# Weights' sums partly by DMA, SwiGLU groups of 8, 6, 8, and later first hidden tiles in a two-layer trunk kernel

## The chip, the cores and the metric

The kernel runs on one core of a Trainium2 chip. The metric is the device time of one execution in microseconds, the median of three runs. In this text TensorE is PE in the rows of the profile, VectorE is DVE, ScalarE is ACT, GpSimd is POOL, and SP is the engine whose queue issues most DMAs. T is 528, the 512 tokens with 16 learned meta tokens ahead of them.

## What is computed

Two layers, each a half-step SwiGLU (f1), a mixer (retention in layer 0, gated linear attention, GLA, in layer 1), and another half-step SwiGLU (f2), all in float32:

```python
def swiglu(x, w_in, w_out):
    gate, up = jnp.split(x @ w_in, 2, axis=-1)
    return (jax.nn.silu(gate) * up) @ w_out

for i in range(DEPTH):                      # D_MODEL 1024, D_FF 2816 = 22 tiles of 128
    h = h + 0.5 * swiglu(rmsnorm(h, norm_ffn1[i]), ffn1_w_in[i], ffn1_w_out[i])
    hn = rmsnorm(h, norm_mix[i])
    h = h + (retention if i % 2 == 0 else gla)(hn, ...)
    h = h + 0.5 * swiglu(rmsnorm(h, norm_ffn2[i]), ffn2_w_in[i], ffn2_w_out[i])
h = rmsnorm(h, final_norm)                  # meta tokens are dropped
```

## The kernel before, in words

All activations lie transposed, features on the 128 partitions and tokens along the free axis, in eight residual tiles x[0..7]. Every float32 operand of a matmul is split into a high part (rounded to fp32r) and a low part (the rest), and one product is three matmuls (`mm3`, lines 311 to 313): high x high, high x low, low x high. So each piece of weights of up to 512 columns costs a copy on ScalarE (`whi`, line 121) and a subtraction on VectorE (`wlo`, line 122).

Most of the work is done in units. A unit multiplies two weight tiles with both halves of the tokens in 7 products in place of 8 (Strassen's scheme in Winograd's form). For that, `Weights` takes four quarters of two loaded weight tiles (a11, a12 in the first, a21, a22 in the second) and forms four sums on VectorE (`ws`, line 107): s1 = a21 + a22, s2 = s1 + a11, s3 = a11 + a21, s4 = a12 + s2. The activations get four such sums too (`t_sums`, lines 463 to 466). The order within a unit is a11, s1, s2, a12, s3, s4, a22; the first unit of a SwiGLU begins with s1 and s2. A product runs over nk pairs of tiles, 3 matmuls each: 84 matmuls in a unit with nk = 4, 63 with nk = 3. There are 134 units, 18 input and 12 output units in each of four SwiGLUs and 14 in the retention.

A SwiGLU computes its first four hidden tiles plainly, straight from the entering residual, while the norm's statistics are still on their way (`plain`, `evac`; the norm is applied to the result). Meanwhile VectorE forms the normed tiles and their sums (`norm`, `sums`). Then pairs of tiles follow as a gate unit and an up unit each. `hidden` splits a finished pair of hidden tiles and forms its sums. Hidden tiles are put into groups (8, 8 and 6 of the 22; in the very last SwiGLU 6, 6, 6 and 4). When a group is full, four output units, each for two residual tiles, are put behind the next gate unit; the last group's follow the last up unit at once. In a SwiGLU that feeds a next stage the last group's output units also carry that stage's entry (`feed`): for each residual tile the scaled high part on ScalarE (`uha`, line 382), the low part on VectorE (`ula`, line 384), a square on ScalarE and the sum of squares on VectorE (`sqa`, line 392). The norm's power is taken on GpSimd (`rc`, line 429; in the heads of the mixers `r_ro` and `r_go`, line 356).

Weights are loaded by SP's queue in DMAs of 1024 columns (512 KB) into four buffers, and split ahead into seven pairs of buffers, up to four pieces ahead of the one in use. Buffers, semaphores and the order of the instructions on each engine come from a planner, which simulates the program with its own costs and issues what is ready by priority; the chip then runs each engine's list in that fixed order. A piece of work marked `urgent` is taken earlier.

Of the kernel before, what the change touches and what calls it, by code (L numbers as in the profile page):

```python
# [10 lines left out]
F32 = mybir.dt.float32  # L11
# [5 lines left out]
P = 128  # L17
# [6 lines left out]
T = 528  # L24
# [5 lines left out]
GROUPS = ((0, 8), (8, 16), (16, 22))  # L30
# [15 lines left out]
CW = 1024  # L46
# [8 lines left out]
class Weights:  # L55

    UNIT = ("a11", "s1", "s2", "a12", "s3", "s4", "a22")
    FIRST = ("s1", "s2", "a11", "a12", "s3", "s4", "a22")  # L60
    SUMS = {"s1": ("a21", "a22"), "s2": ("s1", "a11"), "s3": ("a11", "a21"), "s4": ("a12", "s2")}

    def __init__(self, tc, ctx, raw_bufs=4, bufs=7):
        self.nc = tc.nc
        self.raw_pool = ctx.enter_context(tc.tile_pool(name="wraw", bufs=raw_bufs))
        self.pool = ctx.enter_context(tc.tile_pool(name="wsplit", bufs=bufs))
        self.raw_bufs, self.bufs = raw_bufs, bufs
        self.chunks, self.raw = [], {}
        self.plan, self.parts, self.sums = [], {}, {}
        self.loaded = self.done = self.split = self.taken = 0  # L70
        self.live = set()
        self.sum_pool = None

    def add(self, key, ap):
        n = ap.shape[1]
        c = len(self.chunks)
        self.chunks.append(ap)
        for o in range(0, n, PW):
            self.plan.append((key, c, o, min(PW, n - o), o + PW >= n))

    def add_unit(self, key, ap1, ap2, order):
        c = len(self.chunks)
        self.chunks += [ap1, ap2]
        for q in order:
            self.plan.append((key + (q,), c, q, ap1.shape[1] // 2, {"s4": c, "a22": c + 1}.get(q)))

    def _load(self):
        while self.loaded < min(self.done + self.raw_bufs, len(self.chunks)):
            ap = self.chunks[self.loaded]
            t = self.raw_pool.tile([P, CW], F32, tag="raw", name=f"raw{self.loaded}")  # L90
            self.nc.sync.dma_start(t[:, :ap.shape[1]], ap)
            self.raw[self.loaded] = t
            self.loaded += 1

    def _piece(self, c, q):

        V = self.nc.vector
        if not isinstance(q, str):
            return self.raw[c][:, q:q + PW]
        n = self.chunks[c].shape[1] // 2  # L100
        if q[0] == "a":
            o = (int(q[2]) - 1) * n
            return self.raw[c + int(q[1]) - 1][:, o:o + n]
        if (c, q) not in self.sums:
            a, b = [self._piece(c, i) for i in self.SUMS[q]]
            t = self.sum_pool.tile([P, PW], F32, tag="wsum", name=f"w{q}_{c}")[:, :n]
            V.tensor_add(t, a, b)  # L107
            self.sums[c, q] = t
        return self.sums[c, q]

    def _split(self, upto):
        oldest = min(self.live, default=self.taken)
        upto = min(upto, len(self.plan), oldest + self.bufs)
        while self.split < upto:
            i = self.split
            _, c, q, n, last = self.plan[i]
            self._load()
            raw = self._piece(c, q)
            hi = self.pool.tile([P, PW], F32R, tag="hi", name=f"whi{i}")
            lo = self.pool.tile([P, PW], F32R, tag="lo", name=f"wlo{i}")  # L120
            self.nc.scalar.copy(hi[:, :n], raw[:, :n])  # L121
            self.nc.vector.tensor_sub(lo[:, :n], raw[:, :n], hi[:, :n].bitcast(F32))  # L122
            self.parts[i] = (hi, lo)
            self.split += 1
            if last not in (None, False):
                self.raw.pop(c if last is True else last)
                self.done += 1
                self._load()

    def prime(self, n=None):  # L130
        bufs = self.raw_bufs
        self.raw_bufs = n or bufs
        self._load()
        self.raw_bufs = bufs
# [27 lines left out]
def trunk(ctx, tc, a):  # L162
# [28 lines left out]
    def plan_ffn(w_in, w_out, layer, which, last=False):  # L191
        first = True
        for kind, a_, b_ in ffn_steps(last):
# [7 lines left out]
            else:  # L201
                f0, f1 = (LAST_GROUPS if last else GROUPS)[a_]
                c = slice(f0 * P, f1 * P)
                if kind == "o":
                    W.add_unit(key, w_out[layer, b_, :, c], w_out[layer, b_ + 1, :, c], W.UNIT)
                else:
                    W.add(key, w_out[layer, b_, :, c])
# [58 lines left out]
    W.prime(1)  # L266
# [190 lines left out]
    def t_sums(pool, name, halves, y1, y2, hi, lo):  # L457


        (a0, a1), (b0, b1) = halves  # L460
        wd = a1 - a0
        t = pool.tile([P, 4, 264], F32, tag="su", name=f"tt{name}")[:, :, :wd]
        V.tensor_sub(t[:, 0], y1[:, a0:a1], y1[:, b0:b1])
        V.scalar_tensor_tensor(t[:, 1], y2[:, b0:b1], -1.0, t[:, 0], ALU.mult, ALU.subtract)
        V.tensor_sub(t[:, 2], y2[:, b0:b1], y1[:, b0:b1])
        V.scalar_tensor_tensor(t[:, 3], y2[:, a0:a1], -1.0, t[:, 1], ALU.mult, ALU.subtract)
        split(hi[:, :, :wd], lo[:, :, :wd], t)
# [5 lines left out]
    def unit(key, name, first, halves, nk, rhs, pool, row1, c22, c21):  # L473
# [35 lines left out]
    def quarters(halves, th, tl):  # L509
# [3 lines left out]
        def rhs(what, k):  # L513
# [3 lines left out]
            i = ("t1", "t2", "n3", "t4").index(what)  # L517
# [5 lines left out]
    def ffn(which, layer, halves, gcol, feed, late=False):  # L523
# [5 lines left out]
        with tc.tile_pool(name=f"h_{me}", bufs=4) as hp, tc.tile_pool(name=f"t_{me}", bufs=1) as tp, \  # L529
                tc.tile_pool(name=f"u_{me}", bufs=3) as up_, tc.tile_pool(name=f"s_{me}", bufs=4) as sp, \  # L530
# [1056 lines left out]
```

## Time and profile before

| | us |
|---|---|
| median of 3 runs (2143.5 to 2145.68) | 2143.53 |
| the profiled execution | 2141.96 |
| its span, first to last instruction | 2140.2 |
| TensorE busy, matmuls (16950) | 2103.9 |
| VectorE busy (3451 instructions) | 1868.0 |
| ScalarE busy | 1146.0 |
| GpSimd busy (25 instructions) | 21.8 |

The mean granted clock of TensorE was 0.997 of full. The stages, by windows of the span: head and first SwiGLU to 375 us, retention to 820, second SwiGLU to 1170, third to 1528, GLA to 1800, last SwiGLU to the end. Matmuls overlap: the next begins before the one ahead of it has ended, so that TensorE shows as busy although its beat is slower than it could be; the number of matmuls in a window tells more.

### The profile page before, as it was taken

Reading aid. Unit: us, or ns where it says so; the run is one execution under the profiler, and the core shown is the slowest. Engines: PE = TensorE matmul, PEld = TensorE weight load, DVE = VectorE, ACT = ScalarE, POOL = GpSimd, SP = SyncE. Lnnn points to the kernel's source line nnn. Section 1 sums busy time; section 2 is a strip of 40 time slices with the busy share of each in tenths; the row PEclk is TensorE's granted clock in tenths of the full one; section 3 lists DMA queues with packets and bytes.
Section 4 is the critical chain, followed back from the end, with each engine's and each line's share of the span. In section 5 each row is a group of like instructions: output and inputs, shape, how many; then the busy total and the mean of one; then the engine's idle time right before and its main releaser. Section 6 shows DMA issues by size and latency. Waiting matters only on the chain.

```text
span 2140.2 us, 42535 instructions
## 1 busy us (share of the span) xinstructions
PE 2103.9 (98%) x16950; PEld 2069.3 (97%) x16950; DVE 1868.0 (87%) x3451; ACT 1146.0 (54%) x2220; POOL 21.8 (1%) x25
## 2 busy tenths in 40 slices
PE   8999999999999999999999999999999999999998
PEld 7999999999999999999998999999899999999998
DVE  7999999977686879999999999989876658999996
ACT  5656656443434354656566565656733235656654
POOL 0000000000000000000000000000000000000000
PEclk9999999999999999999999999999999999999999
DMA  4333323332222222232323233332312112233332
GB/s 142 98 110 100 103 93 92 100 110 82 97 80 96 83 71 79 90 109 99 109 93 96 80 109 103 97 107 86 122 60 66 63 62 78 87 121 99 104 109 75
DMA packets 59175, 201.26 MB, mean 94 GB/s; under 512 B 6624, under 2 KB 8032, under 8 KB 58976
## 3 DMA queue, kind: packets, MB, share of 16 engines
q1 hardware_dynamic: 57968, 195.26, 28.5%
q10 hardware_dynamic: 1008, 3.29, 0.5%
q8 instruction: 133, 2.18, 0.4%
q14 instruction: 66, 0.54, 0.1%
HBM read 196.42 MB, written 2.10 MB: 93 GB/s over the span
## 4 chain that ended last, share of the span: by engine, by line
PE 79%; DVE 15%; ACT 2%; DMA 2%; issue 2%; POOL 0%; SPq 0%; DVEq 0%; POOLq 0%; ACTq 0%
DVE wlo L122 4%; DVE ws L107 2%; PE po_r L313 1%; PE po_r L311 1%; PE po_r L312 1%; PE lv L1227 1%; DVE hf L340 1%; PE Xf21o L311 1%; PE Xf20o L311 1%; DMA raw<-in_f_in 1%; PE Xf20g L311 1%; PE Xf20g L312 1%; PE Xf20g L313 1%; PE Xf20u L311 1%; PE Xf11g L311 1%
## 5 line engine op out<-in xcount | busy, mean ns | idle before, releaser
L121 ACT CAST whi<-raw 128x512 fp32r<-128x512 f32 (+1 forms) x613 | 369.1, 608 | 393.2 <-PE gv L312 51.0
L121 ACT CAST whi<-ws 128x512 fp32r<-128x512 f32 (+1 forms) x536 | 322.3, 603 | 340.9 <-DVE ws L107 86.8
L122 DVE TENSOR_TENSOR wlo<-raw,whi 128x512 fp32r<-128x512 f32 (+1 forms) x613 | 402.9, 668 | 67.6 <-ACT whi L121 65.8
L122 DVE TENSOR_TENSOR wlo<-ws,whi 128x512 fp32r<-128x512 f32 (+1 forms) x536 | 349.5, 659 | 27.6 <-ACT whi L121 25.5
L107 DVE TENSOR_TENSOR ws<-raw 128x512 f32<-128x512 f32 (+1 forms) x134 | 88.6, 661 | 20.1 <-DMA raw<-in_f_in 13.6
L107 DVE TENSOR_TENSOR ws<-ws,raw 128x512 f32<-128x512 f32 (+1 forms) x134 | 88.6, 661 | 1.6
L107 DVE TENSOR_TENSOR ws<-raw,raw 128x512 f32<-128x512 f32 (+1 forms) x134 | 88.3, 659 | 0.4
L107 DVE TENSOR_TENSOR ws<-raw,ws 128x512 f32<-128x512 f32 (+1 forms) x134 | 88.2, 658 | 0.4
L313 PE MATMUL po_r<-ogh,wlo 128*128 128x264 f32 x256 | 72.9, 285 | 0.0
L311 PE MATMUL po_r<-ogh,whi 128*128 128x264 f32 x256 | 72.9, 285 | 0.0
L312 PE MATMUL po_r<-ogl,whi 128*128 128x264 f32 x256 | 72.6, 284 | 0.0
L339 ACT CAST hf<-yf 128x264 fp32r<-128x264 f32 (+2 forms) x86 | 45.0, 534 | 33.0 <-DVE yf L641 20.3
L311 PE MATMUL Xf10o<-hf,whi 128*128 128x264 f32 x176 | 51.1, 291 | 2.9 <-ACT whi L121 2.7
L311 PE MATMUL Xf11o<-hf,whi 128*128 128x264 f32 x176 | 51.1, 291 | 2.9 <-ACT whi L121 2.7
L311 PE MATMUL Xf20o<-hf,whi 128*128 128x264 f32 x176 | 51.1, 291 | 2.8 <-ACT whi L121 2.7
L313 PE MATMUL Xf20o<-hf,wlo 128*128 128x264 f32 x176 | 50.3, 286 | 0.0
L313 PE MATMUL Xf11o<-hf,wlo 128*128 128x264 f32 x176 | 50.3, 286 | 0.0
L313 PE MATMUL Xf10o<-hf,wlo 128*128 128x264 f32 x176 | 50.3, 286 | 0.0
L312 PE MATMUL Xf10o<-hf,whi 128*128 128x264 f32 x176 | 50.1, 285 | 0.0
L312 PE MATMUL Xf11o<-hf,whi 128*128 128x264 f32 x176 | 50.0, 285 | 0.0
L312 PE MATMUL Xf20o<-hf,whi 128*128 128x264 f32 x176 | 50.0, 285 | 0.0
L340 DVE TENSOR_TENSOR hf<-yf,hf 128x264 fp32r<-128x264 f32 (+2 forms) x86 | 49.3, 573 | 0.6 <-ACT hf L339 0.5
(732 smaller groups left out, 8671.6 us busy)
## 6 DMA issues: line engine op xcount, KB each, us to landing
raw<-in_f_in SPq DMA_DIRECT2D x176, 512.0 KB, 3.5
raw<-in_f_out SPq DMA_DIRECT2D x48, 512.0 KB, 3.6
raw<-in_ret_in SPq DMA_DIRECT2D x48, 512.0 KB, 3.4
raw<-in_f_out SPq DMA_DIRECT2D x48, 384.0 KB, 3.1
raw<-in_gla_in SPq DMA_DIRECT2D x25, 512.0 KB, 3.4
raw<-in_ret_o SPq DMA_DIRECT2D x16, 512.0 KB, 3.4
raw<-in_gla_o SPq DMA_DIRECT2D x8, 512.0 KB, 3.5
xa<-in_xT SPq DMA_DIRECT2D x8, 264.0 KB, 5.3
```

The costliest lines, as they stand in the source:

```text
L107: V.tensor_add(t, a, b)
L121: self.nc.scalar.copy(hi[:, :n], raw[:, :n])
L122: self.nc.vector.tensor_sub(lo[:, :n], raw[:, :n], hi[:, :n].bitcast(F32))
L311: nc.tensor.matmul(ps, lhsT=lh, rhs=rh, start=start, stop=False, **kw)
L312: nc.tensor.matmul(ps, lhsT=lh, rhs=rl, start=False, stop=False, **kw)
L313: nc.tensor.matmul(ps, lhsT=ll, rhs=rh, start=False, stop=stop, **kw)
L339: S.copy(hi, src)
L340: V.tensor_sub(lo, src, hi.bitcast(F32))
L1227: nc.tensor.matmul(ps[:, j, J * P:J * P + n], lhsT=Kt[:, j, J * P:(J + 1) * P], rhs=q, start=(J == 0), stop=(J == 3), skip_group_check=True)
```

## The change

Weights of units are loaded in smaller pieces: the quarters a11, a12 and a22 as tiles of their own (seven buffers of 512 columns), and a pair tile (three buffers) that gets a11 and a22 by SP's queue and then a21 added to both halves by one accumulating DMA of GpSimd's queue. The pair is then s3 and s1. VectorE still forms s2 and s4, in place, right after the split of a11 and a12. A pair is begun no more than three units ahead of the split.

The groups become 8, 6, 8. The last group's first output unit runs its first three products (order a11, s1, a12) over all pairs of tiles but the last, then over the last.

Of the first four, plain hidden tiles, the splits and sums are put behind the next gate units (`todo`). The sums of activations are three instructions in place of four, and a hidden tile is split in two pieces in place of three. Plain weights are loaded in DMAs of 512 columns. The scratch for GpSimd's DMAs is 2048 in place of 4096.

```diff
-GROUPS = ((0, 8), (8, 16), (16, 22))
+GROUPS = ((0, 8), (8, 14), (14, 22))
...
+    LATE = ("a11", "s1", "a12", "s2", "s3", "s4", "a22")
+    def __init__(self, tc, ctx, raw_bufs=7, pair_bufs=3, bufs=7):
...
     def add_unit(self, key, ap1, ap2, order):
+        a = {"a11": ap1[:, :n], "a12": ap1[:, n:], "a21": ap2[:, :n], "a22": ap2[:, n:]}
+        self.loads["pair"].append((c, len(self.plan), (a["a11"], a["a22"], a["a21"])))
+        for q in ("a11", "a12", "a22"):
+            self.loads["raw"].append(((c, q), len(self.plan), (a[q],)))
...
     def _load(self):
+        for kind, loads in self.loads.items():
+            while self.begun[kind] < min(self.over[kind] + self.room[kind], len(loads)):
+                c, first, aps = loads[self.begun[kind]]
+                if kind == "pair" and first > self.split + 3 * len(self.UNIT):
+                    break
+                if kind == "pair":
+                    t = self.pair_pool.tile([P, 2, PW], F32, tag="pair", name=f"pair{c}")[:, :, :n]
+                    for i in range(2):
+                        nc.sync.dma_start(t[:, i], aps[i])
+                    nc.gpsimd.dma_start(t, aps[2].unsqueeze(1).broadcast_to([P, 2, n]), accum_op=ALU.add)
+                else:
+                    t = self.raw_pool.tile([P, PW], F32, tag="raw", name=f"raw{self.begun[kind]}")[:, :n]
+                    nc.sync.dma_start(t, aps[0])
...
     def _split(self, upto):
+                late = order[0] == "s1"
+                s2 = self.tiles[c][:, 1] if late else self.tiles[c, "a11"]
+                raw = {"s1": self.tiles[c][:, 1], "s3": self.tiles[c][:, 0], "s2": s2,
+                       "s4": self.tiles[c, "a12"]}.get(q)
...
+            self.nc.scalar.copy(hi[:, :n], raw)
+            V.tensor_sub(lo[:, :n], raw, hi[:, :n].bitcast(F32))
+                if q == ("s1" if late else "a11"):
+                    V.tensor_add(s2, self.tiles[c][:, 1], self.tiles[c, "a11"])
+                elif q == "a12":
+                    V.tensor_add(raw, raw, s2)
...
-    def t_sums(pool, name, halves, y1, y2, hi, lo):
+    def t_sums(pool, name, b22_b11, b12, b21):
+        V.tensor_sub(t[:, :2], b22_b11, b12.unsqueeze(1).broadcast_to([P, 2, wd]))
+        V.scalar_tensor_tensor(t[:, 2], b22_b11[:, 0], -1.0, t[:, 1], ALU.mult, ALU.subtract)
+        V.scalar_tensor_tensor(t[:, 3], b21, -1.0, t[:, 2], ALU.mult, ALU.subtract)
...
     def unit(key, name, order, halves, nk, rhs, pool, row1, c22, c21):
+        steps = [(q, 0, nk) for q in order]
+        if order == W.LATE:
+            steps = [(q, 0, nk - 1) for q in order[:3]] + [(q, nk - 1, nk) for q in order[:3]] + steps[3:]
...
             def hidden(f, y):
-                    split(hi[:, 4], lo[:, 4], y[:, 0, a0:a1])
-                    t_sums(up_, f"{me}h{f}", halves, y[:, 0], y[:, 1], h[:, 0, :4], h[:, 1, :4])
-                    split(hi[:, 5:], lo[:, 5:], pair(y[:, 1], halves))
+                    t = t_sums(up_, f"{me}h{f}", y[:, 1:3], y[:, 3], y[:, 0])
+                    split(hi[:, :3], lo[:, :3], y[:, :3])
+                    split(hi[:, 3:], lo[:, 3:], t)
...
             def evac(f, outs):
-                    hidden(f - 1, y)
+                    todo.append((f - 1, y))
...
+                    while todo and (a_ == "g" or b_ + 2 == groups[0][1]):
+                        hidden(*todo.popleft())
+                        if a_ == "g":
+                            break
```

## Rows read from the trace of the kernel before

**Rows 1.** The page, busy time and share of the span of each engine.
```profile
PE 2103.9 (98%) x16950; PEld 2069.3 (97%) x16950; DVE 1868.0 (87%) x3451; ACT 1146.0 (54%) x2220; POOL 21.8 (1%) x25
```

**Rows 2.** Windows: width; busy (instructions) of PE, PEld, DVE, ACT, POOL; clock, DMA share, GB/s.
```profile
1340.00:1380.00 40.00, 40.00 (x331) 40.00 (x330) 39.46 (x72) 25.95 (x52) 0.00 (x0) 1.00 0.33 107
2080.00:2100.00 20.00, 20.00 (x172) 20.00 (x171) 17.27 (x30) 12.54 (x26) 0.00 (x0) 1.00 0.28 80
60.00:320.00 260.00, 259.54 (x2113) 257.78 (x2113) 247.46 (x441) 154.37 (x305) 0.00 (x0) 1.00 0.31 100
1200.00:1480.00 280.00, 279.79 (x2281) 278.10 (x2280) 266.86 (x476) 166.67 (x324) 0.00 (x0) 1.00 0.33 102
1800.00:2100.00 300.00, 299.77 (x2506) 297.61 (x2506) 296.07 (x562) 183.38 (x375) 0.00 (x0) 1.00 0.32 99
```

**Rows 3.** Windows in the head, at a group's end and in last output units.
```profile
48.00:62.00 14.00, 9.29 (x53) 8.76 (x53) 12.06 (x24) 4.90 (x7) 0.00 (x0) 0.76 0.25 77
56.00:58.00 2.00, 2.00 (x11) 2.00 (x11) 2.00 (x5) 0.80 (x2) 0.00 (x0) 0.50 0.88 283
336.00:344.00 8.00, 7.37 (x50) 6.28 (x50) 8.00 (x17) 5.47 (x13) 0.00 (x0) 1.00 0.16 50
358.00:370.00 12.00, 9.79 (x70) 8.76 (x70) 11.83 (x24) 7.50 (x17) 0.00 (x0) 1.00 0.28 91
1510.00:1528.00 18.00, 14.67 (x106) 13.18 (x105) 17.71 (x35) 13.49 (x29) 0.00 (x0) 1.00 0.39 121
```

**Rows 4.** Waits: engine and line, whom it waited for, us in total, times, longest.
```profile
ACT whi L121 <- DVE ws L107: 86.8, 69, 3.4
...
PE Xf10o L311 <- ACT whi L121: 2.7, 3, 1.2
```

**Rows 5.** The page's groups of instructions: the sums s1 and s3 on VectorE.
```profile
L107 DVE TENSOR_TENSOR ws<-raw 128x512 f32<-128x512 f32 (+1 forms) x134 | 88.6, 661 | 20.1 <-DMA raw<-in_f_in 13.6
...
L107 DVE TENSOR_TENSOR ws<-raw,raw 128x512 f32<-128x512 f32 (+1 forms) x134 | 88.3, 659 | 0.4
```

**Rows 6.** Groups of instructions on VectorE from 346 to 376 us.
```profile
L384 DVE SCALAR_TENSOR_TENSOR ula<-xa,gains,uha 128x528 fp32r<-128x528 f32 x8 | 6.0, 761 | 0.0
...
L665 DVE SCALAR_TENSOR_TENSOR xa<-QZf10o,xa 128x528 f32<-128x528 f32 x4 | 2.8, 701 | 0.2 <-PE QZf10o L313 0.2
...
L676 DVE SCALAR_TENSOR_TENSOR xa<-Xf10o,xa 128x264 f32<-128x264 f32 x4 | 1.7, 429 | 0.0
```

**Rows 7.** Timeline of VectorE: start, us, line, operation, out<-in.
```profile
355.53 0.70 DVE L392 TENSOR_TENSOR sqa_n<-sqa_n,sq_n 128x528 f32<-128x528 f32 x1
...
358.42 0.55 DVE L107 TENSOR_TENSOR ws<-raw,raw 128x384 f32<-128x384 f32 x1
...
359.82 1.01 DVE L122 TENSOR_TENSOR wlo<-ws,whi 128x384 fp32r<-128x384 f32 x2
...
380.31 1.88 DVE L122 TENSOR_TENSOR wlo<-raw,whi 128x512 fp32r<-128x512 f32 x3
```

**Rows 8.** Timeline of TensorE and VectorE at a group's end, and at 359 us.
```profile
335.94 0.28 PE L313 MATMUL Xf10u<-thf,wlo 128*128 128x264 f32 x1
...
340.40 1.25 DVE L340 TENSOR_TENSOR hf<-ttf10h,hf 128x1056 fp32r<-128x1056 f32 x1
...
341.70 0.19 PEld L312 LDWEIGHTS QZf10o<-hf,whi 128*128 128x128 f32 x1 [0.27 <-DVE hf L340]
...
359.56 0.39 PE L311 MATMUL Xf10o<-hf,whi 128*128 128x264 f32 x1 [1.22 <-ACT whi L121]
```

**Rows 9.** Timeline of VectorE in the head.
```profile
46.54 1.24 DVE L340 TENSOR_TENSOR hf<-ttf10h,hf 128x1056 fp32r<-128x1056 f32 x1
...
51.48 0.68 DVE L122 TENSOR_TENSOR wlo<-raw,whi 128x512 fp32r<-128x512 f32 x1
```

**Rows 10.** The page's DMA issues: count, KB each, median us to landing.
```profile
raw<-in_f_in SPq DMA_DIRECT2D x176, 512.0 KB, 3.5
```

**Rows 11.** Timeline of POOL at the first SwiGLU's end.
```profile
378.20 1.90 POOL L429 TENSOR_TENSOR rc<-ms_n,half_neg 128x4 f32<-128x4 f32 x2 [354.56 <-DVE ms_n L427]
```

More of the change, by code (lines that the diff above doesn't have):

```diff
@@ L66, in __init__ @@
         self.pool = ctx.enter_context(tc.tile_pool(name="wsplit", bufs=bufs))
[L67 to L70, printed above, removed]
+        self.bufs = bufs
+        self.loads = {"raw": [], "pair": []}
+        self.begun = dict.fromkeys(self.loads, 0)
+        self.over = dict.fromkeys(self.loads, 0)
+        self.room = {"raw": raw_bufs, "pair": pair_bufs}
@@ L71, in __init__ @@
+        self.tiles, self.plan, self.parts = {}, [], {}
+        self.split = self.taken = self.keys = 0
         self.live = set()
-        self.sum_pool = None
     def add(self, key, ap):
[L75 to L79, printed above, removed]
-    def add_unit(self, key, ap1, ap2, order):
-        c = len(self.chunks)
-        self.chunks += [ap1, ap2]
+        c = self.keys
@@ L84, in add_unit @@
         for q in order:
-            self.plan.append((key + (q,), c, q, ap1.shape[1] // 2, {"s4": c, "a22": c + 1}.get(q)))
+            self.plan.append((key + (q,), c, q, n, order))
     def _load(self):
[L88 to L93, printed above, removed]
@@ L95, in _piece @@
-    def _piece(self, c, q):
-        V = self.nc.vector
[L98 to L109, printed above, removed]
@@ L204, in plan_ffn @@
                 if kind == "o":
-                    W.add_unit(key, w_out[layer, b_, :, c], w_out[layer, b_ + 1, :, c], W.UNIT)
+                    late = not last and (a_, b_) == (len(GROUPS) - 1, 0)
+                    W.add_unit(key, w_out[layer, b_, :, c], w_out[layer, b_ + 1, :, c], W.LATE if late else W.UNIT)
                 else:
@@ L537, in ffn, with place @@
             groups = GROUPS if feed else LAST_GROUPS
+            def place(j):
+                if j not in normed:
+                    t = hp.tile([P, 4 * T + 4 * 264], F32, tag="H", name=f"un{me}{j}")
+                    normed[j] = t[:, :4 * T].rearrange("p (i h t) -> p i h t", i=2, h=2)
+                    normed[j, "y"] = t[:, 4 * T:].rearrange("p (q t) -> p q t", q=4)
+                return normed[j]
             def norm(j):
-                t = normed[j] = hp.tile([P, 2, 2, T], F32, tag="H", name=f"un{me}{j}")
+                t = place(j)
                 for h in range(2):
@@ L558, in renorm @@
                         k = 4 * h + 2 * j
[L559 removed]
+                        split(uha[:, k:k + 2, r0:r1], ula[:, k:k + 2, r0:r1], normed[j][:, :, 1 - h, r0:r1])
             def gates(f):
@@ L564, in gated @@
             def gated(f):
-                return up_.tile([P, 2, T], F32, tag="su", name=f"y{me}{f}")
+                if f < NPL:
+                    place(f // 2)
+                    return normed[f // 2, "y"][:, :, :wd]
+                return up_.tile([P, 4, 264], F32, tag="su", name=f"y{me}{f}")[:, :, :wd]
             def hidden(f, y):
@@ L571, in hidden @@
                     h = hp.tile([P, 2, 2, T], F32R, tag="H", name=f"h{me}{f}")
-                    split(h[:, 0, :, a0:], h[:, 1, :, a0:], y[:, :, a0:])
+                    for i in range(2):
+                        split(pair(h[:, 0, i, :], halves), pair(h[:, 1, i, :], halves), y[:, 2 - 2 * i:4 - 2 * i])
                 else:
@@ L630, in c21 @@
                     S.activation(g[1][:, a0:a1], c, AF.Silu)
-                unit((which, layer, "i", "g", f), f"{me}g{f}", first, halves, 4, rhs_in, up_, row1, c22, c21)
+                unit((which, layer, "i", "g", f), f"{me}g{f}", W.FIRST if first else W.UNIT, halves, 4, rhs_in, up_,
+                     row1, c22, c21)
                 return g
@@ L678, in c21 @@
                         feed(d + 1, ins)
-                unit((which, layer, "o", gi, d), f"{me}o{gi}{d}", False, halves, len(hs), rhs, up_, row1, c22, c21)
+                late = feed and (gi, d) == (len(groups) - 1, 0)
+                unit((which, layer, "o", gi, d), f"{me}o{gi}{d}", W.LATE if late else W.UNIT, halves, len(hs), rhs,
+                     up_, row1, c22, c21)
             first, ps, outs, g = True, {}, {}, None
```

136 lines of the change are left out of this document (76 added, 60 removed).

## The prediction

> **What bounds the kernel now.** I read the page first: TensorE is busy 98% of the span and VectorE 87% [rows 1]. A busy TensorE is no measure of waste here, since matmuls overlap, so I counted them. In the cleanest stretch that I found, 40 us hold 331 matmuls [rows 2]; one lasts 0.28 us [rows 8], so some 2.3 of those counted only reach over an edge, and the beat is 40 / 328.7 = 0.1217 us for 264 columns. In the last SwiGLU, with 256 columns, 20 us hold 172: 20 / 169.7 = 0.1179 us [rows 2]. The change alters no count of matmuls (the groups are 8, 6, 8 for 8, 8, 6, in all 22 tiles), so all that it can win is time in which the beat is missed: width less (count - 2.3) x beat.
>
> By windows, of three long stretches of SwiGLU units the first (60 to 320) misses 260 - 2110.7 x 0.1217 = 3.1 us and the last (1200 to 1480) 2.7; with as much for the one between them (820 to 1120) and 300 - 2503.7 x 0.1179 = 4.8 us in the last SwiGLU [rows 2] that is 13, spread thin. Short windows give the rest [rows 3]: 7.8 us in the head (48 to 62); 2.2 us where the last group's first output unit begins (336 to 344; there are three such places, the others at 1130 and 1488, so some 6.5 in all); and in the last output units of a SwiGLU that feeds a next stage 3.8 us (358 to 370) and 5.4 (1510 to 1528), with one such place between them some 14 in all. The sum is 7.8 + 6.5 + 14 + 13 = 41 us: 1.9% of the time, and the ceiling.
>
> What ends these misses? The waits name the split of the weights: an output unit's first product waits for the high part, and ScalarE, which makes it, waited 86.8 us for the sums of weights on VectorE [rows 4]. In the short windows VectorE is full (17.71 of 18 us, 11.83 of 12) [rows 3].
>
> **The sums by DMA.** Four sums a unit (s1, s2, s3, s4) become two, since s1 and s3 are now formed as a22 + a21 and a11 + a21 by a DMA that adds to a loaded pair. Taken from VectorE: 134 of each, 88.6 + 88.3 = 177 us of busy time [rows 5]. Instructions in a row overlap a little: three splits of 512 take 1.88 us, so one costs (1.88 - 0.68) / 2 = 0.60 and 268 of them 161 us [rows 5, 7]. In units of 10.2 us (84 matmuls at 0.1217) that is 1.2 us less of VectorE. But there TensorE misses only 1% to 1.6%, so nearly all of the 161 us lies beside other work. Of the 13 us I take back 4 (bounds 0 and 13): short waits for evacuations and splits, of which a VectorE with 12% of air should lose some.
>
> **Groups 8, 6, 8.** In the last group's output units VectorE also carries the next stage's entry. For one unit: two ula at 0.76, two sqa at 0.70, two residual updates of 528 at 0.70, three of 264 at 0.43 [rows 6, 7], each less 0.08 of overlap: 1.36 + 1.24 + 1.24 + 1.05 = 4.9 us. With three pairs the weights are 384 wide; a split or sum costs 1.01 - 0.55 = 0.46 [rows 7], and 7 splits + 4 sums make 5.1. Together 10.0 us, against 63 matmuls x 0.1217 = 7.7 on TensorE: VectorE is 2.3 us short in each of four units, which prefetched splits cover in part, and 14 us in three stages is what is left. The sight of it: squares' sums and weights' sums run at 355.53 and 358.42, and TensorE gets its high part at 359.56, 1.22 us idle [rows 7, 8]. After the change the last group has four pairs: 4.9 + 9 x 0.60 = 10.3 us against the 10.2 of 84 matmuls. The shortage falls from 2.3 to 0.1 us. I take back 11 of 14 us (bounds 0 and 14). The middle group, now of three pairs, pays nothing: without the entry its units ask 2.3 + 9 x 0.46 = 6.4 us of VectorE in 7.7.
>
> **The last group's first unit begun without its last tiles.** Before, the last up-unit's last matmul starts at 335.94, VectorE splits the sums of its hidden tile from 340.40 to 341.65, and TensorE, which ran what it could, waits for them at 341.70 [rows 8]: 5.6 us of chain, of which 2.2 are missed. Merged sums hardly shorten it (four of 0.35 become one of 0.62 and two of 0.35; three splits become two): 0.2 us. The new order runs three products over three of four pairs first, 27 matmuls or 3.3 us, then the fourth pair's two plain products (0.36 each): 4.0 us. If the planner lets s2's first products in as well, the wait goes; if not, 1.6 us stay. I take 1.3 a place, 4 of 6.5 us (0 and 6.5). Its price: three weights must lie split within 3.3 us where one per 1.1 to 1.4 us did; should they be late, it is this gain that goes.
>
> **The first hidden tiles split later.** In the head VectorE does norms, their sums and the first two hidden tiles one behind the other. A weight's low part comes only at 51.48, behind, among others, the hidden tile's split at 46.54 [rows 9], while TensorE stands and its granted clock falls, to a mean of 0.76 over 48 to 62 and to half, the 1.2 GHz level, at 56 [rows 3]. Moving hidden tile 0 behind the first gate unit takes away four sums of 264 (1.4 together, at 0.43 less overlap), splits of 264 and 528 (1.0, at the same prices [rows 6]) and of 1056 (1.2 [rows 9]), some 3.5 us. The stand is about 4.5 us, and the clock's fall follows it; with 1 us left I expect no fall (the wait at 359 left the clock at 1.00 [rows 3]). Back: 5 of 7.8 us (0 and 7.8). The moved work lands in units that have 1.2 us of new air each; three units take it.
>
> **What it adds.** In each of 134 units: two pair loads and three quarters of 256 KB each on SP's queue (less where a unit is 384 wide) in place of two loads of 512 KB, and one accumulating DMA on POOL's queue, that writes 512 KB and reads its source twice. The trace has no such DMA and none from POOL. It waits for its two loads; behind it on POOL stand the next pair's DMA and the small powers of the norms, behind its landing the splits of s1 and s3 on ScalarE and VectorE. Nearest row: 512 KB plain lands in 3.5 us [rows 10]; so the chain of a pair is 3.5 for the loads and between 3.5 and, at five times that, 17 us for the add. Pairs are begun about three units (30 us) ahead, so even 21 us is covered; without that cover each unit would wait. The DMA engines are 0.33 busy in a stretch where a unit loads 1 MB [rows 2]; 1.25 MB plain is 0.41, and the add 0.17 at the plain price, its lower bound: 0.58 at least, full enough to collide. The upper bound is five times that, rival B below; by the nearest row I take the lower one. The Trainium skill ("Collectives: The Full Stack", The bandwidth ceiling: the fold count and why AG ≠ RS ≠ AR) speaks against a cheap add: a DMA that sums reads two sources over one ring, so it moves half of what a copy does. By that rule the add would take 0.33 and the engines would be 0.74 busy, and the time would still be TensorE's; no run here shows its rate yet. Plain weights in DMAs of half the size and the smaller scratch I cost at nothing: they are loaded seven pieces ahead, about 2.9 us of matmuls each, against 3.5 us to land; without that lead a stage's first pieces would wait. For POOL's queue, later loads and a new order of all queues I put 3 us (bounds 0 and 15; a gain is excluded, since nothing is taken from these queues).
>
> **Sum.** 4 + 11 + 4 + 5 - 3 = 21 us. Against the profiled execution: 2141.96 - 21 = 2121.0 (its span is 2140.2, 1.8 us lie around it); the median of the runs is 1.6 us above it, so I forecast 2122.5 us.
>
> **Rivals.** (A) The order hardly changes: VectorE's order is fixed ahead by the planner, which put entry work before weights' splits when both were ready [rows 7]; if it does so again, the freed time lies between stalls and not in them, and I lose most of 11 + 5, leaving some 5 us: 2138.5. For it: VectorE idles almost nowhere in the stalls. Against it: there the demand itself was too high, and that falls. Chance 0.15.
>
> (B) Slower: the add is so dear that the DMA engines bind. It decides where a unit's DMA time passes 10.2 us: 4.2 us plain (0.41 x 10.2) leaves 6.0 for the add, that is 3.5 times its plain 1.7 us. At four times: 4.2 + 6.8 = 11.0, 0.8 us a unit x 134 = 107, less the 21 won: 2230; at five times 2.5 x 134 = 335, and 2458. For it: no row gives an add's rate. Against it: engines at a third. Chance 0.07.
>
> (C) Slower: POOL's queue. A norm's power (two take 1.90 us [rows 11]) stands behind a pair's DMA that waits for its loads, 3.5 us; 14 such norms (6 of stages, 8 of heads), uncovered, are 49 us less the 21: 2143.5 + 28 = 2171. For it: POOL serves in order. Against it: most norms have matmuls under them. Chance 0.06.
>
> **Numbers.** Forecast 0.72. All terms at their best give 41 us back; the three local ones whole (28) and most of the thin 13 give 39, the low end: 2104. (A) is held by a top end of 2140; B and C lie outside (0.13). Within 0.2% (4.3 us) is about what a measurement of this kernel cannot tell from no change: faster than that 0.80, within 0.08 (half of A), slower 0.12.
>
> **What would show it.** Right: two sums a unit on VectorE, its share in the long stretches near 0.84 for 0.95; over 330 matmuls per 40 us in stretches that had fewer; no fall of the clock at 50 us; under 2 us missed in the last units of a stage. Wrong: TensorE or ScalarE waiting for a pair's DMA in mid-stage (B), a POOL power late with matmuls idle (C), or VectorE full with the same waits (A). Shares of DMA above 0.8 would speak for B.

## The result, and the profile after

The changed kernel took 2117.39 us (median of 4 runs, 2117.36 to 2117.42) against 2143.52 for the kernel before (2143.41 to 2145.68): a ratio of 0.9876, with a 95% interval of 0.9864 to 0.9889. The forecast was 2122.5, with a range of 2104 to 2140. The profiled span fell from 2140.2 to 2115.3 us, by 24.9.

The page after: engines, then DMA queues (packets, MB, share of 16 engines' span), and the issues of weights (count, KB, us to landing).

```profile
PE 2090.6 (99%) x16950; PEld 2064.2 (98%) x16950; DVE 1731.8 (82%) x3085; ACT 1143.5 (54%) x2184; POOL 184.7 (9%) x159
...
q1 hardware_dynamic: 130400, 228.84, 33.0%
q0 software_dynamic: 36448, 67.12, 20.0%
...
raw<-in_f_in SPq DMA_DIRECT2D x280, 256.0 KB, 4.0
pair<-in_f_in SPq DMA_DIRECT2D x144, 256.0 KB, 4.6
pair<-in_f_in POOLq DMA_DIRECT2D x72, 512.0 KB, 6.2
```

The count of matmuls is the same as in [rows 1], so again all that was won is time in which the beat is missed: width less (count - 2.3) x 0.1217 us, or x 0.1179 in the last SwiGLU. Windows after, with the columns of [rows 2]: the head; the last output units of the first three SwiGLUs; the three groups' ends; the long stretches of the four SwiGLUs.

```profile
48.00:62.00 14.00, 14.00 (x117) 14.00 (x116) 13.28 (x20) 7.54 (x15) 0.00 (x0) 1.00 0.29 95
338.00:362.00 24.00, 24.00 (x200) 24.00 (x199) 22.52 (x41) 16.28 (x33) 1.21 (x1) 1.00 0.68 172
1128.00:1154.00 26.00, 25.62 (x211) 25.42 (x209) 24.80 (x44) 18.57 (x37) 2.55 (x3) 1.00 0.67 182
1478.00:1504.00 26.00, 25.53 (x207) 25.08 (x206) 24.66 (x43) 18.72 (x38) 2.42 (x2) 1.00 0.72 189
317.00:330.00 13.00, 12.08 (x94) 11.45 (x93) 10.90 (x19) 6.51 (x13) 1.20 (x1) 1.00 0.73 174
1107.00:1120.00 13.00, 12.25 (x95) 11.62 (x94) 11.00 (x19) 6.75 (x13) 1.22 (x1) 1.00 0.70 173
1460.00:1473.00 13.00, 12.25 (x95) 11.61 (x94) 10.88 (x19) 7.96 (x16) 1.20 (x1) 1.00 0.52 123
60.00:320.00 260.00, 259.78 (x2123) 258.79 (x2122) 232.02 (x399) 159.97 (x312) 31.49 (x26) 1.00 0.70 178
810.00:1100.00 290.00, 290.00 (x2372) 289.11 (x2371) 256.06 (x435) 172.37 (x330) 30.30 (x25) 1.00 0.64 162
1180.00:1460.00 280.00, 280.00 (x2293) 279.34 (x2292) 245.13 (x419) 168.10 (x324) 31.50 (x26) 1.00 0.68 172
1770.00:2070.00 300.00, 299.22 (x2502) 296.88 (x2500) 269.81 (x485) 180.99 (x361) 32.69 (x27) 1.00 0.63 161
```

| place | missed before | missed after | won | forecast |
|---|---|---|---|---|
| head, 48 to 62 us | 7.8 | 0.0 | 7.8 | 5 |
| last output units, three stages | 14 | 0, 0.6, 1.1 = 1.7 | 12.3 | 11 |
| first output unit of the last group, three places | 6.5 | 1.8 + 1.7 + 1.7 = 5.3 | 1.2 | 4 |
| long stretches, thin | 13 | 1.9 + 1.6 + 1.2 + 5.3 = 10.0 | 3.0 | 4 |
| what the change adds, and the rest | | | 0.6 | -3 |

The four places hold 24.3 of the 24.9 us. In the head (first line) 117 matmuls stand where [rows 3] had 53, at a clock of 1.00 for 0.76. At a group's end (lines 5 to 7) little was won. Measured between the norms' powers on POOL, the retention took 441.0 us before and 440.95 after, GLA 261.4 and 260.4, and the last SwiGLU with the final norm 348.5 and 348.8: nearly all of the gain lies in the first three SwiGLUs (12.7, 5.4 and 6.8 us). The retention and the last SwiGLU got the sums by DMA too, but no new groups, and they are no faster.

### The profile page after: what moved, and what is told of

Same layout as the page of the kernel before. It is cut to its first block, busy times and chain, and to the rows that moved or that the text cites. A ratio compares the mean times of both kernels' runs of the same rounds, so it can differ in the third digit from the quotient of the medians.

```text
span 2115.3 us, 43783 instructions
## 1 busy us (share of the span) xinstructions
PE 2090.6 (99%) x16950; PEld 2064.2 (98%) x16950; DVE 1731.8 (82%) x3085; ACT 1143.5 (54%) x2184; POOL 184.7 (9%) x159
## 3 DMA queue, kind: packets, MB, share of 16 engines
q1 hardware_dynamic: 130400, 228.84, 33.0%
q0 software_dynamic: 36448, 67.12, 20.0%
## 4 chain that ended last, share of the span: by engine, by line
PE 94%; DVE 3%; ACT 1%; DMA 1%; issue 0%; POOL 0%; SPq 0%; POOLq 0%; DVEq 0%; ACTq 0%
PE po_r L335 1%; PE po_r L336 1%; PE po_r L337 1%; PE lv L1282 1%; PE Xf20o L335 1%; PE Xf11o L335 1%; PE Xf10o L335 1%; PE Xf20o L336 1%; PE Xf11o L336 1%; PE Xf21o L335 1%; PE Xf11o L337 1%; PE Xf20o L337 1%; PE Xf10o L336 1%; PE Xf10o L337 1%; PE Xf11g L335 1%; PE Xf20g L335 1%
## 5 line engine op out<-in xcount | busy, mean ns | idle before, releaser
L136 ACT CAST whi<-raw 128x512 fp32r<-128x512 f32 (+1 forms) x877 | 519.7, 606 | 589.4 <-DVE raw L142 64.2
L137 DVE TENSOR_TENSOR wlo<-raw,whi 128x512 fp32r<-128x512 f32 (+1 forms) x877 | 574.6, 668 | 194.7 <-ACT whi L136 182.4
L136 ACT CAST whi<-pair 128x512 fp32r<-128x512 f32 (+1 forms) x272 | 163.7, 602 | 146.4 <-PE po_r L336 13.7
L137 DVE TENSOR_TENSOR wlo<-pair,whi 128x512 fp32r<-128x512 f32 (+1 forms) x272 | 179.9, 661 | 11.8 <-ACT whi L136 10.4
L111 POOL DMA_DIRECT2D pair<-in_f_in x72 | 87.4, 1214 | 733.4 <-DVE wlo L137 249.2
L111 POOL DMA_DIRECT2D pair<-in_f_out x48 | 58.1, 1211 | 463.0 <-DVE wlo L137 213.1
L142 DVE TENSOR_TENSOR raw<-pair,raw 128x512 f32<-128x512 f32 (+1 forms) x130 | 86.3, 664 | 2.6
L144 DVE TENSOR_TENSOR raw<-raw,raw 128x512 f32<-128x512 f32 (+1 forms) x130 | 86.2, 663 | 2.5
L337 PEld LDWEIGHTS po_r<-ogh,wlo 128*128 128x128 f32 x256 | 48.2, 188 | 0.0
L335 PEld LDWEIGHTS po_r<-ogh,whi 128*128 128x128 f32 x256 | 48.1, 188 | 0.0
```

The source lines that it names most:

```text
L111: nc.gpsimd.dma_start(t, aps[2].unsqueeze(1).broadcast_to([P, 2, n]), accum_op=ALU.add)
L136: self.nc.scalar.copy(hi[:, :n], raw)
L137: V.tensor_sub(lo[:, :n], raw, hi[:, :n].bitcast(F32))
L142: V.tensor_add(s2, self.tiles[c][:, 1], self.tiles[c, "a11"])
L144: V.tensor_add(raw, raw, s2)
L335: nc.tensor.matmul(ps, lhsT=lh, rhs=rh, start=start, stop=False, **kw)
```

## The experiments

Each kernel was timed in five rounds beside the kernel before. The base of those that change the changed kernel is that kernel run once more: 2119.03 us (2116.47 to 2121.10; ratio 0.9892, interval 0.9879 to 0.9906) in the rounds and on the chip of two kernels below (groups and later hidden tiles; the last hidden tile split in the order of its products). There its granted clock fell briefly at two stage entries (a mean of 0.91 from 362 to 382 and from 1142 to 1162 us), which it did not in the first profile (1.00 in both); two of its four executions took 2116.47 and 2117.58, the other two 2120.48 and 2121.10. So a difference of 2 to 4 us against this base is not clear by the times alone.

> The changed kernel once more, on the chip and in the rounds of the two kernels beside it, as their base: 2117 to 2119 by every theory.

**Groups undone.**

```
-GROUPS = ((0, 8), (8, 14), (14, 22))
+GROUPS = ((0, 8), (8, 16), (16, 22))
```

> The changed kernel, but with the groups of 8, 8, 6 tiles of the kernel before. Theory 1 (the short last group makes VectorE late): with two sums a unit in place of four, VectorE is asked 4.9 + 9 x 0.46 = 9.0 us in a last output unit that gives TensorE 7.7, short by 1.3 where it was short by 2.3, so 1.3 / 2.3 of the 14 us come back, about 8: 2125 us, with fewer than 160 matmuls per 20 us in the last output units of the three stages. Theory 2 (VectorE was relieved enough by the sums' DMA, the groups add nothing): 2117 to 2119, and the last output units as full as in the changed kernel.

2134.66 us, ratio 0.9961 (0.9949 to 0.9974): 15.6 slower, twice what theory 1 said, and theory 2 falls. The last output units miss again, and the next stage's entry with them: 28 - 187.7 x 0.1217 = 5.2 us in one stage. The window, then VectorE, ScalarE and TensorE in it:

```profile
344.00:372.00 28.00, 25.25 (x190) 23.23 (x188) 25.16 (x47) 18.45 (x38) 2.42 (x2) 1.00 0.66 184
```

```profile
344.08 0.55 DVE L137 TENSOR_TENSOR wlo<-pair,whi 128x384 fp32r<-128x384 f32 x1
...
346.24 1.44 DVE L408 SCALAR_TENSOR_TENSOR ula<-xa,gains,uha 128x528 fp32r<-128x528 f32 x2
347.59 1.51 DVE L416 TENSOR_TENSOR sqa_n<-sqa_n,sq_n 128x528 f32<-128x528 f32 x2
...
349.37 1.02 DVE L137 TENSOR_TENSOR wlo<-raw,whi 128x384 fp32r<-128x384 f32 x2
```

```profile
342.61 0.52 ACT L136 CAST whi<-pair 128x384 fp32r<-128x384 f32 x1
...
348.15 0.93 ACT L136 CAST whi<-raw 128x384 fp32r<-128x384 f32 x2
```

```profile
348.72 0.39 PE L335 MATMUL Xf10o<-hf,whi 128*128 128x264 f32 x1 [1.15 <-ACT whi L136]
```

TensorE's long wait here (1.15 us) is for ScalarE, which has a block of entry work of its own: no copy of a weight begins between 342.61 and 348.15, 5.5 us.

**Groups alone, on the kernel before.**

```
-GROUPS = ((0, 8), (8, 16), (16, 22))
+GROUPS = ((0, 8), (8, 14), (14, 22))
```

> The kernel before, with nothing but the groups changed to 8, 6, 8 (all four sums of a unit on VectorE). Theory 1 (each part alone wins its part): VectorE is asked 4.9 + 11 x 0.60 = 11.5 us in a last output unit that gives TensorE 10.2, short by 1.3 where it was 2.3: 14 x 1.0 / 2.3 = 6 us won, 2137. Theory 2 (the groups win only together with the sums by DMA, since a last group of four pairs asks as much more of VectorE as it gives TensorE): 2141 to 2145. Theory 3 (the groups do it alone): 2131.

2124.49 us, ratio 0.9915 (0.9902 to 0.9927): 18 us won by this line alone, more than any of the three theories had. The last output units are whole (32 - 259.7 x 0.1217 = 0.4 us missed), though all four sums are on VectorE and it is busy 31.49 of 32 us; the head stays bad (6.2 us missed, at a clock of 0.76). At the groups' ends it misses 1.8, 1.7 and 1.7 us, as the changed kernel does, though it has the old order and the unmerged sums. Windows (last output units, head, first group's end), then VectorE in the last unit:

```profile
330.00:362.00 32.00, 31.89 (x262) 31.68 (x261) 31.49 (x56) 21.87 (x43) 0.00 (x0) 1.00 0.25 81
48.00:62.00 14.00, 10.38 (x66) 9.93 (x65) 13.47 (x26) 5.73 (x9) 0.00 (x0) 0.76 0.23 77
323.00:336.00 13.00, 12.11 (x94) 11.49 (x93) 12.53 (x24) 7.24 (x15) 0.00 (x0) 1.00 0.32 95
```

```profile
355.77 0.68 DVE L122 TENSOR_TENSOR wlo<-raw,whi 128x512 fp32r<-128x512 f32 x1
...
360.85 0.68 DVE L122 TENSOR_TENSOR wlo<-ws,whi 128x512 fp32r<-128x512 f32 x1
```

Between those two splits VectorE does 5.1 us of entry work, updates and sums, and TensorE misses nothing. With three pairs gaps of the same length end in a stall: 5.3 us from 344.08 to 349.37 on VectorE and 5.5 on ScalarE, above. The difference may be what lies ahead: splits run four products ahead, and four products of four pairs are 48 x 0.1217 = 5.8 us of matmuls, of three pairs 36 x 0.1217 = 4.4. No run varied that lead by itself.

**Hidden tiles at once.**

```
-                    todo.append((f - 1, y))
+                    hidden(f - 1, y)
```

> The changed kernel, but each of the first hidden tiles is split as soon as it is there, as before the change. Theory 1 (the head's stand came of that order): 5 to 8 us slower, 2122 to 2125, with the granted clock below 1 between 48 and 62 us again. Theory 2 (the head was mended by the sums that moved to DMA): 2117 to 2119, and the clock stays at 1.00.

2120.80 us, ratio 0.9898 (0.9885 to 0.9912): 1.8 above the base, which the times don't tell from nothing. In its trace 48 to 62 us holds 102 matmuls for 117, at a clock of 1.00: 14 - 99.7 x 0.1217 = 1.9 us missed. Nearer theory 2: of the 6.2 us that the head misses with the groups alone, 4.3 were mended without the later split.

**Groups and later hidden tiles, all sums on VectorE.**

```
-GROUPS = ((0, 8), (8, 16), (16, 22))
+GROUPS = ((0, 8), (8, 14), (14, 22))
...
-                    hidden(f - 1, y)
+                    todo.append((f - 1, y))
...
+                    while todo and (a_ == "g" or b_ + 2 == groups[0][1]):
+                        hidden(*todo.popleft())
```

> The kernel before with two parts of the change: groups of 8, 6, 8, and the first hidden tiles split one unit later each (their gated values kept beside the normed tile, as in the changed kernel). All four sums of a unit stay on VectorE, and the hidden tile's sums stay unmerged. With the groups alone the head still missed 6.2 us between 48 and 62 us, at a clock of 0.76. Theory 1 (in the head either cure is enough, and the sums by DMA win little elsewhere): the head is whole, the clock 1.00, 2118 to 2120. Theory 2 (the head was mended by the sums' DMA alone): 2123 to 2125, the head as with the groups alone.

2124.49 us, ratio 0.9917 (0.9904 to 0.9931): nothing against the groups alone. Each theory has one half: the time is theory 2's, but the head is nearly whole, as theory 1 had it. What is won there is lost right behind it. Windows of this kernel, then of the groups alone:

```profile
48.00:62.00 14.00, 12.67 (x102) 12.24 (x101) 13.98 (x23) 7.26 (x13) 0.00 (x0) 1.00 0.24 77
82.00:102.00 20.00, 18.94 (x151) 18.27 (x150) 19.87 (x37) 13.30 (x27) 0.00 (x0) 1.00 0.21 60
102.00:122.00 20.00, 18.63 (x146) 17.91 (x147) 19.78 (x36) 12.39 (x26) 0.00 (x0) 1.00 0.36 109
```

```profile
82.00:102.00 20.00, 19.64 (x161) 19.43 (x160) 19.96 (x37) 12.67 (x26) 0.00 (x0) 1.00 0.33 108
102.00:122.00 20.00, 20.00 (x166) 20.00 (x166) 19.93 (x36) 12.80 (x27) 0.00 (x0) 1.00 0.35 104
```

The head wins 4.4 us (102 matmuls for 66, worth 36 x 0.1217), and the next 40 us lose 30 matmuls, 3.7 us: the moved work lands on a VectorE that is full (19.87 and 19.78 of 20 us). In the changed kernel VectorE has some air there (19.26 and 18.91 of 20), and no matmul is missed from 82 to 122 us (167 and 166).

**The last group's first unit in the ordinary order.**

```
-W.LATE if late else W.UNIT
+W.UNIT
```

> The changed kernel, but the last group's first output unit in the ordinary order. Theory 1 (the wait is set by the hidden tile's chain and by the weights' split buffers, and the planner already fills it with other products, so the new order wins next to nothing): 2117 to 2119, the same 1.7 to 1.9 us missed at each group's end. Theory 2 (as forecast, 1.3 us a place): 4 us slower, 2121.

2122.81 us, ratio 0.9904 (0.9891 to 0.9918): 3.8 above the base, as theory 2 says, though the intervals overlap; the trace decides. In the three windows of 13 us at a group's end it misses 4.4, 4.4 and 2.9 us, where the changed kernel misses 1.8, 1.7 and 1.7. At each of them TensorE now waits 1.05 us for the low part of the last hidden tile's plain quarters; at two of the three its granted clock then falls (320 to 326 us here), at the third, after the same wait, it stays at 1.00 (last line):

```profile
320.00:322.00 2.00, 0.59 (x3) 0.39 (x3) 1.17 (x3) 0.76 (x2) 0.34 (x1) 1.00 0.72 239
322.00:324.00 2.00, 2.00 (x11) 2.00 (x12) 1.97 (x3) 1.12 (x2) 0.86 (x1) 0.60 0.31 42
324.00:326.00 2.00, 2.00 (x11) 2.00 (x11) 0.48 (x1) 0.00 (x0) 0.00 (x0) 0.54 0.94 147
1460.00:1473.00 13.00, 11.21 (x85) 10.37 (x84) 11.00 (x19) 6.80 (x13) 1.20 (x1) 1.00 0.79 183
```

```profile
PE Xf10o L336 <- DVE hf L364: 1.1, 1, 1.1
```

So the new order is worth some 4 us (1.2 a place without the clock's fall). But it only repays what another part of the change costs: with the groups alone, in this same old order, the three places miss 5.2 us in all, as much as in the changed kernel (5.3). Here are VectorE and TensorE at the group's end in the changed kernel, where the last up-unit's last matmul starts at 317.48:

```profile
320.30 0.98 DVE L364 TENSOR_TENSOR hf<-yf,hf 128x792 fp32r<-128x792 f32 x1
...
322.45 0.69 DVE L137 TENSOR_TENSOR wlo<-raw,whi 128x512 fp32r<-128x512 f32 x1 [0.83 <-ACT whi L136]
323.18 0.69 DVE L142 TENSOR_TENSOR raw<-pair,raw 128x512 f32<-128x512 f32 x1
323.79 1.25 DVE L364 TENSOR_TENSOR hf<-ttf10h,hf 128x1056 fp32r<-128x1056 f32 x1
```

```profile
321.33 0.39 PE L336 MATMUL Xf10o<-hf,whi 128*128 128x264 f32 x1 [0.18 <-DVE hf L364]
...
322.48 0.39 PE L335 MATMUL Xf10o<-hf,whi 128*128 128x264 f32 x1 [0.63 <-ACT whi L136]
```

The sums' low parts end at 325.04, 7.6 us after that matmul; before it was 341.65 - 335.94 = 5.7 [rows 8] (5.6 in the prediction), and with the groups alone, where weights are 512 wide, 6.5. The merged split of 792 lets the first plain quarter come only with the third, 3.8 us after that matmul (2.5 with the groups alone), and a split and a sum of the next unit's weights stand ahead of the sums' split. TensorE's own waits are for that plain part (0.18 us) and then for a weight's high part (0.63), which waits for a free buffer, as the kernel with eight of them shows below; with the groups alone that second wait is the same.

**The last hidden tile split in the order of its products.** This follows from it.

```
+                    end = feed and f + 2 == groups[-1][1]
+                    if end:
+                        split(hi[:, 2], lo[:, 2], y[:, 2])
                     t = t_sums(...)
-                    split(hi[:, :3], lo[:, :3], y[:, :3])
+                    if not end:
+                        split(hi[:, :3], lo[:, :3], y[:, :3])
                     split(hi[:, 3:], lo[:, 3:], t)
+                    if end:
+                        split(hi[:, :2], lo[:, :2], y[:, :2])
```

> The changed kernel, but the last hidden tile of a group of outputs that feeds a next stage is split in the order in which its products come: its first quarter by itself (264), then the merged sums, then their split, and the other two quarters last. Theory 1 (the merged split of 792 and a weight's split stand ahead of the sums' split in the chain of 7.6 us from the last matmul to the sums' low parts, and this chain ends last): the chain is 1.5 to 2 us shorter, 0.3 to 0.8 us missed per group's end in place of 1.8: 3 to 5 us faster than the changed kernel, 2112 to 2115. Theory 2 (the split buffers that three held weights keep end last): 2116 to 2118.

2115.90 us (2114.93 to 2116.26), ratio 0.9877 (0.9864 to 0.9891): 3.1 below its base in the same rounds; the ranges of the two don't meet, their intervals overlap. It is the fastest kernel of the study. The first plain quarter's low part now ends 2.3 us after the last matmul (319.15 against 316.84) and the sums' low parts 6.0 (322.85):

```profile
316.84 0.28 PE L337 MATMUL Xf10u<-thf,wlo 128*128 128x264 f32 x1
...
321.61 0.39 PE L335 MATMUL QZf10o<-hf,whi 128*128 128x264 f32 x1 [0.86 <-ACT hf L363]
```

```profile
318.72 0.43 DVE L364 TENSOR_TENSOR hf<-yf,hf 128x264 fp32r<-128x264 f32 x1
...
321.59 1.26 DVE L364 TENSOR_TENSOR hf<-ttf10h,hf 128x1056 fp32r<-128x1056 f32 x1 [0.54 <-ACT hf L363]
```

```profile
316.00:329.00 13.00, 12.14 (x98) 11.74 (x96) 12.16 (x22) 6.91 (x14) 1.20 (x1) 1.00 0.72 173
```

The wait that is left is for ScalarE's high part of the sums. In windows of 13 us 98, 99 and 99 matmuls stand for 94, 95 and 95: 1.3 us missed a place for 1.8. The chain shrank as expected, the misses fell less than theory 1 had it (to 0.3 to 0.8). The three places hold some 1.5 of the 3.1 us; the base's clock falls at stage entries, which this profile doesn't have, are a likely part of the rest.

**Eight split buffers, and the plain buffers for the room.** Two kernels: five plain buffers alone, and five with eight split buffers.

```
-raw_bufs=7, pair_bufs=3, bufs=7
+raw_bufs=5, pair_bufs=3, bufs=7
```

> The changed kernel with five plain buffers of weights in place of seven, nothing else: how far the lead of plain loads matters. Theory 1 (five pieces of 1.1 to 1.5 us each lead by 6 to 7 us, more than the 4.0 us that a piece takes to land): 2117 to 2120. Theory 2 (the lead is what keeps splits on time, and it was it that cost the kernel with VectorE's sums its 57 us): 2140 or more, ScalarE waiting for plain loads.

2121.85 us, ratio 0.9900 (0.9886 to 0.9915): some 3 us slower than the base, on another chip and within the intervals. The lead of plain loads is no part of the large losses.

```
-raw_bufs=7, pair_bufs=3, bufs=7
+raw_bufs=5, pair_bufs=3, bufs=8
```

> The changed kernel with eight split buffers in place of seven (and five plain ones, for the room). Theory 1 (at a group's end TensorE waits 0.6 and 0.4 us for splits whose buffers the three weights held there keep): against the kernel with seven split and five plain buffers 1 to 1.6 us less at each of three places, 3 to 5 us faster; the wait of the first output product for ScalarE's high part (0.6 us each) is gone. Theory 2 (the hidden tile's own chain on VectorE ends last, a buffer more only moves the wait to it): within 1.5 us of that kernel.

2130.93 us, ratio 0.9946 (0.9934 to 0.9958): 9 us slower than with seven, so both theories miss the time. At the groups' ends theory 1 is right: the waits for a weight's high part are gone, and each of the three places misses 0.6 us in place of 1.7 to 1.8 (first line), though the sums' low parts still end 7.3 us after the last matmul. So that chain costs only what TensorE has no other product for. The loss is at stage entries, where TensorE waits for ScalarE's high parts of the new input: ahead of them on ScalarE stands a weight's split, which waits 2.0 to 3.3 us for its load:

```profile
320.60:333.60 13.00, 13.00 (x104) 12.58 (x103) 11.63 (x21) 7.32 (x14) 1.20 (x1) 1.00 0.48 109
```

```profile
PE pg_gz L1205 <- ACT uha L406: 3.4, 1, 3.4
PE pf11g L335 <- ACT uha L406: 2.4, 1, 2.4
PE pq L335 <- ACT uha L406: 1.6, 1, 1.6
```

**The sums by DMA taken away.** In the first try each sum was formed on VectorE right ahead of its own split; s2 and s4 were formed from a pair not yet added, so only its time is read.

```
-                    nc.gpsimd.dma_start(t, aps[2]..., accum_op=ALU.add)
+                    nc.sync.dma_start(o, aps[2])
...
+                if q in ("s1", "s3"):
+                    V.tensor_add(self.tiles[c][:, j], self.tiles[c][:, j], self.third[c])
```

> The changed kernel, but s1 and s3 are added by VectorE again (two adds more per unit, the third quarter loaded plainly into a tile of its own; for its room five plain buffers in place of seven), with groups 8, 6, 8 kept. Theory 1 (both are needed in the last output units): VectorE is asked 10.3 + 1.2 = 11.5 us in units that give TensorE 10.2, short by 1.3, so some 8 of the 12.3 us won there and the 3 us won in the long stretches are lost: 2128. Theory 2 (the groups alone did it): 2120, only the long stretches lose. Theory 3 (the adding DMA costs something elsewhere that its absence gives back): below 2117.

2174.48 us, ratio 1.0147 (1.0133 to 1.0160), far past every theory. ScalarE waited 213 us for those adds, each put right ahead of its split: the run measures sums that come too late, not VectorE's load. The second try forms both sums ahead of the unit's first split (`if q == order[0]:`).

> The changed kernel, but with s1 and s3 added on VectorE from three plainly loaded quarters, both adds before the unit's first split (not each ahead of its own split, as in the first try), and five plain buffers. Its base is the changed kernel with five plain buffers, 2121.85. Theory 1 (the sums by DMA give the air on VectorE that the merged and moved work lands in): 4 to 8 us slower than that, 2126 to 2130, with misses in the first units after the head and in the long stretches, where VectorE is over 0.93 busy again. Theory 2 (the groups were nearly all, the sums by DMA win nothing): 2121 to 2123.

2137.99 us, ratio 0.9976 (0.9966 to 0.9987): 16 slower than with five plain buffers (on another chip), at least twice theory 1. A long stretch, and the last output units:

```profile
820.00:1100.00 280.00, 276.09 (x2243) 273.67 (x2242) 263.60 (x459) 160.42 (x308) 0.00 (x0) 1.00 0.43 138
330.00:362.00 32.00, 31.90 (x262) 31.76 (x260) 31.63 (x56) 22.37 (x46) 0.00 (x0) 1.00 0.32 103
```

The long stretch misses 280 - 2240.7 x 0.1217 = 7.3 us where the changed kernel misses 1.6 in 290; the last output units stay whole. Part of it must be this arrangement (both adds ahead of the unit's first split, three loads): the kernel before, with the same four sums and groups 8, 6, 8, takes 2124.49. Against that kernel with later hidden tiles the rest of the change (the DMA sums, the merged sums, the new order and the smaller loads together) is worth 2124.49 - 2119.03 = 5.5 us. No run takes the DMA sums alone away.

**Each adding DMA twice.**

```
+                    nc.gpsimd.dma_start(t, aps[2].unsqueeze(1).broadcast_to([P, 2, n]), accum_op=ALU.add)
```

> The changed kernel, but each adding DMA is issued twice in a row on POOL's queue (so the third quarter goes twice into s1 and s3). The DMA engines were 0.70 busy from 60 to 320 us where the kernel before had 0.31; its plain loads grew by a quarter, to 0.39, so one add takes 0.31, near the rule that an adding DMA moves half of what a copy does. Theory 1 (that rate): 1.01 of a unit's 10.2 us, so the DMA engines just bind: 0 to 3% slower than the changed kernel in the units, 2117 to 2160, DMA share above 0.9, and waits for a pair's DMA on ScalarE and VectorE. Theory 2 (the second add costs as a plain load, 0.17): share 0.87, the time stays at 2117 to 2119.

2271.34 us, ratio 1.0601 (1.0576 to 1.0626): 152 slower, past theory 1, and theory 2 falls. What bounds it is POOL's queue: the second add waits 8.0 us (553.9 / 69) for the first to land, and with two issues of 1.2 to 1.7 us and short waits between pairs its queue takes 11.2 us a pair (four pairs from 101.16 to 145.96 us), for a unit of 10.2.

```profile
POOL pair L112 <- DMA pair<-in_f_in: 553.9, 69, 11.0
POOL pair L112 <- DMA pair<-in_f_out: 355.2, 51, 10.5
```

DMA engines were 0.88 busy from 60 to 300 us, and TensorE's clock fell there to a mean of 0.96. So the slowdown of rival B appears with a second add, and through POOL's queue, with the engines near full but not full; with one add it does not (a share of 0.70, 1.9 us missed in 260).

## Why the prediction was right, and where not

**What bounds the kernel.** The count of the beat held: 24.3 of 24.9 us lie in the four places named. Of the two waits that were named for them, TensorE's for a weight's high part did fall (from 2.7 to 0.6 us for the output products of a stage). ScalarE's 86.8 us of waiting for VectorE's sums [rows 4] did not: they are 90.7 with the groups alone and 91.3 in the changed kernel (64.2 + 20.6 + 6.5), so most of that total cost TensorE nothing.

**Groups 8, 6, 8** was the right place and nearly the right size (12.3 of 14, forecast 11), for a wrong reason. That the groups are the cause is shown, by the edit alone and by its undoing: 18 us and 15.6, the largest part of the change. The balance of VectorE against TensorE doesn't decide: by its prices both trials are 1.3 us a unit short (9.0 against 7.7 with groups 8, 8, 6 and two sums; 11.5 against 10.2 with 8, 6, 8 and four), and one misses 5 us in a stage and the other 0.4. What may differ is how long one block of entry work may be: the prediction's own rows are of such a block [rows 7], no split begun on VectorE between 354.39 and 359.82, and its 5.4 us are longer than the 4.4 of four short products. That reading fits the traces of the kernel before, the changed kernel and both trials; that it is the cause was argued, not isolated.

**The first hidden tiles split later** was mis-sized, and the working credited it with what several parts do together: 5 was forecast, 7.8 came. The groups alone took 1.6 of that. With the rest of the change the later split is worth 1.9 us in the head; without that rest it wins 4.4 us there and loses 3.7 in the next 40 us. The prediction's sentence that the moved work lands in units with new air names what it needs.

**The sums by DMA** and what came with them (merged sums, smaller loads) mend the other 4.3 us of the head; how much of that is the DMA sums alone, no run shows. In the long stretches 3.0 came for 4, part of it by the groups: from 60 to 320 us 3.1 us are missed before, 2.3 with the groups alone and 1.9 after. The last SwiGLU won nothing (5.3 us missed for 4.8). VectorE's share in the long stretches is 0.88 to 0.90, not 0.84: its busy time fell by 136 us, not 161.

**The last group's first unit begun without its last tiles** is the term that failed: 1.2 us for 4, and the groups alone bring as much (5.2 us missed, against 5.3). The edit itself gives what was forecast (3.8 when undone). The step that failed is "merged sums hardly shorten it": they lengthen the chain, to 7.6 us for 6.5 with the groups alone and 5.7 before, and the first plain quarter comes 3.8 us after the last matmul. Costs were added up instruction by instruction, and not in the order in which the parts are used. That 1.7 to 1.8 us stayed a place, near the 1.6 of the prediction's "if not", is chance: the chain is 2 us longer than in that sum, and other products fill part of it.

**What it adds** was put at -3 and is about nothing: in the changed kernel ScalarE and VectorE wait 7 us in all for a pair's DMA, TensorE not at all, and the norms' powers are on time, so rival C falls. Rival A, freed time that misses the stalls, falls too: 12.3 and 7.8 us came out of them. For the add I took the plain price, 0.17 of the engines, and 0.58 in all; 0.70 was measured (60 to 320 us). Its queue moved 67.12 MB in 20.0% of the span, SP's loads 228.84 MB in 33.0%: 0.298 against 0.144% per MB, 2.1 times as dear. The rule of the Trainium skill ("Collectives: The Full Stack", The bandwidth ceiling: the fold count and why AG ≠ RS ≠ AR), that a DMA which sums reads two sources and moves half of what a copy does, agrees with this; that page states it for the reduce step of a ring between cores.

**The sum** came near, 21 us for 24.9, partly by luck: the head and what the change adds were 2.8 and 3.6 us better than forecast, the last output units 1.3, and the groups' ends and the long stretches 2.8 and 1.0 worse.

## What to carry to other kernels

Ask of a stall not only whether an engine has enough time over the whole stage, but how long its longest block of other work is against the work that lies split ahead. A wait of one helper engine for another is a cost only where TensorE runs out of products; count the misses in a short window before the wait is blamed. Air on an engine pays where something else is moved into it, so measure two such edits together and apart. Merge operations where they are off the path; where TensorE waits for the first part, split in the order in which the parts are used.

## What was not expected of the hardware

- In the ordinary order TensorE stood for two waits of 1.05 and 0.63 us within 2.5 us (319.44 to 321.91); the granted clock then fell to the 1.2 GHz level (0.54 from 324 to 326 us, matmuls 0.22 us apart for 0.12). At another group's end the same two waits left it at 1.00, as did the shorter ones of the changed kernel.
- An adding DMA of 512 KB lands in 6.2 us and takes 1.21 us of POOL to issue; with DMA engines 0.70 busy from 60 to 320 us TensorE missed 1.9 us.
- More room was no help in sum: an eighth split buffer won about 1.1 us at each of three groups' ends and the kernel lost 9 us.
